# A Mamba-2 and attention trunk: the gate blocks read x's tokens, or write their columns, in another order

## The chip, the cores and the metric

The kernel runs on one NeuronCore of one Trainium2 chip. The metric is device time in microseconds, the median of several runs of the same program. A profile is one execution, taken by the hardware profiler.

## What is computed

The reference is a two-layer decoder trunk on x of 256 tokens by 2048 channels. The first layer is a Mamba-2 mixer, the second a sliding-window attention; each ends in a LayerNorm. The change touches the first projection of the first layer alone, and of it the part called z:

```python
zxbcdt = x @ w_in                                  # x: 256 x 2048
z = zxbcdt[..., :D_INNER]                          # D_INNER = 4096
xbc = zxbcdt[..., D_INNER:D_INNER + CONV_DIM]      # x, B and C of the state-space part
...
y = y.reshape(bsz, seqlen, D_INNER) * jax.nn.silu(z.astype(jnp.float32))
yg = y.reshape(bsz, seqlen, SSM_GROUPS, D_INNER // SSM_GROUPS)
yg = yg * lax.rsqrt(jnp.mean(jnp.square(yg), axis=-1, keepdims=True) + EPS)
```

So z is 4096 channels by 256 tokens, and silu of z gates the state-space output y, channel by channel and token by token.

## The kernel before

All weights come from HBM as fp32, in units of 128 x 2048. `load_unit` brings a unit in two DMAs (tile `wr`), ScalarE rounds it to fp32r (L133, tile `wh`) and VectorE takes the remainder (L134, tile `wl`). x is split once in the same way into `xH` and `xL`. A product is then three matmuls in `mac` (L195 to L197): high by high, high by low, low by high, all summed in PSUM.

The projection runs in eight groups of ten blocks. A block is one unit of weights, 128 output channels: for each of the 16 tiles of 128 input channels, `mac` holds 128 x 128 weights in the array and streams the 256 tokens of x, so a block is 48 matmuls of 256 columns into one PSUM tile `mm` (a ring of four). Channels lie on partitions and tokens along the row. The blocks of a group are B, C, four of xs and four of z (numbers 6 to 9, which the code calls i = 0 to 3); in group 0 the z blocks come first, and the very first of them shares its loop with the block of dt while the weights still come in. x lies in SBUF as rows of 256 fp32r tokens for each tile of 128 channels (`Split`), so a matmul of L195 reads 1024 contiguous bytes of each partition.

B, C and xs go through a short convolution (`conv_silu`: L357 on ScalarE, three L359 on VectorE). A z block goes through `in_z`: ScalarE reads PSUM and writes tanh to SBUF (L428), VectorE reads that and PSUM and makes the silu (L429). GpSimd multiplies y with z later (`gate`, L492). Between the blocks of groups 1 to 7 stand the output projection's units of the group before (`out_unit`, L255 to L257, 24 matmuls of 512 columns, added to `xr` by VectorE in L262).

The instructions are put in order on each engine by a scheduler that reads priorities; `in_z` is recorded with a raised priority (ZPRI). Group tasks (`cb`, `tr`, `ymm`, `gate`, `norm`) are placed behind given blocks by a table. Units are loaded two ahead of their use.

Of the kernel before, what the change touches and what calls it, by code (L numbers as in the profile page):

```python
# [11 lines left out]
AF = mybir.ActivationFunctionType  # L12
ALU = mybir.AluOpType
AX = mybir.AxisListType

P = 128
S = 256
D = 2048
KT = D // P
# [16 lines left out]
BLOCKS = list(range(10))  # L36
BLOCKS0 = [6, 7, 8, 9, 0, 1, 2, 3, 4, 5]
# [20 lines left out]
def trunk(ctx: ExitStack, tc: tile.TileContext, A: dict, out: bass.AP, dbg=None):  # L58
    nc = tc.nc
# [16 lines left out]
    def nm(s):  # L76
        uid[0] += 1
        return f"{s}_{uid[0]}"

    def mm_tile():  # L80
        return mm_ps.tile([P, 512], F32, tag="mm", name=nm("mm"), bufs=4)
# [38 lines left out]
    def load_unit(src, places):  # L120
        u = new_unit(places)
        raws = []
        for c in range(2):
            raw = wp.tile([P, 1024], F32, tag="wr", name=nm("wr"), bufs=NR)
            nc.sync.dma_start(raw[:], src[:, c * 1024 : (c + 1) * 1024])
            raws.append(raw)
        for c in range(2):
            for (h, k0, k1), (l, _, _) in zip(*u.parts):
                a, b = max(k0, 8 * c), min(k1, 8 * c + 8)
                if a < b:  # L130
                    sl = slice((a - k0) * P, (b - k0) * P)
                    raw = raws[c][:, (a - 8 * c) * P : (b - 8 * c) * P]
                    nc.scalar.activation(h[:, sl], raw, AF.Copy)  # L133
                    nc.vector.tensor_tensor(l[:, sl], raw, h[:, sl].bitcast(F32), ALU.subtract)  # L134
        return u

    def load_first():

        us = [new_unit([WHOLE, WHOLE]) for _ in range(2)]
        for k0, k1 in FIRST:  # L140
            n = k1 - k0
            if n < 3:
                raw = wp.tile([P, 2, 512], F32, tag="wr", name=nm("first"), bufs=NR)
            else:
                raw = ap.tile([P, 3, 512], F32, tag="e", name=nm("first"), bufs=2)
            raw = raw[:, :n, :]
            nc.sync.dma_start(raw, A["first"][:, k0:k1, :])
            nc.scalar.activation(xH(k0, k1), raw[:, :, :S], AF.Copy)
            nc.vector.tensor_tensor(xL(k0, k1), raw[:, :, :S], xH(k0, k1).bitcast(F32), ALU.subtract)
            for i, u in enumerate(us):  # L150
                h, l = [p[:, k0 * P : k1 * P].rearrange("p (k c) -> p k c", c=P) for p in (u.h, u.l)]
                w = raw[:, :, S + i * P : S + (i + 1) * P]
                nc.scalar.activation(h, w, AF.Copy)  # L153
                nc.vector.tensor_tensor(l, w, h.bitcast(F32), ALU.subtract)
        return us
# [23 lines left out]
    def next_unit():  # L179
        if not units:  # L180
            units.extend(load_first())
            nc.sync.dma_start(pc[:], A["pc"])
        while len(units) < min(used[0] + 1 + AHEAD, len(srcs)):
            if len(units) == 5:
                nc.sync.dma_start(cc[:], A["cc"])
            if len(units) in (8, 9):
                i = len(units) - 8
                nc.sync.dma_start(xr[:, i, :], A["xk"][:, i, :])
                nc.scalar.activation(xr[:, i, :], xr[:, i, :], AF.Copy, scale=ALPHA)
            units.append(load_unit(srcs[len(units)], BROKEN if len(units) in broken else [WHOLE, WHOLE]))  # L190
        used[0] += 1
        return units[used[0] - 1]

    def mac(ps, ah, al, bh, bl, first, last):
        nc.tensor.matmul(ps, ah, bh, start=first, stop=False)  # L195
        nc.tensor.matmul(ps, ah, bl, start=False, stop=False)  # L196
        nc.tensor.matmul(ps, al, bh, start=False, stop=last)  # L197
# [49 lines left out]
    xH = Split("xH", 1, 0, 192)  # L247
    xL = Split("xL", 1, 64, 192)
# [17 lines left out]
    def out_last(aH, aL, rms, stats, done):  # L266
# [12 lines left out]
            stats(1, nb)  # L279
        done(1)  # L280

    def gemm_ws(us):
        pss = [mm_tile() for _ in us]
        for k0, k1 in FIRST:
            for ps, u in zip(pss, us):
                for k in range(k0, k1):
                    ks = slice(k * P, (k + 1) * P)
                    mac(
                        ps[:, :S], u.h[:, ks], u.l[:, ks], xH(k, k + 1)[:, 0, :], xL(k, k + 1)[:, 0, :],
                        k == 0, k == KT - 1,  # L290
                    )
        return pss
# [127 lines left out]
    def in_xs(g, i, ps):  # L420
        xs = ap.tile([P, S], F32, tag="sm", name=nm("xs"), bufs=NSM)
        conv_silu(ps, g * 6 + 2 + i, xs[:])
        gs[g].__dict__.setdefault("xs", {})[i] = xs

    def in_z(g, i, ps):
        z = ap.tile([P, S], F32, tag="zz", name=nm("z"), bufs=4)
        with tc.high_priority(ZPRI):
            nc.scalar.activation(z[:], ps[:, :S], AF.Tanh, scale=0.5)  # L428
            nc.vector.scalar_tensor_tensor(z[:], z[:], 1.0, ps[:, :S], ALU.add, ALU.mult)  # L429
        gs[g].__dict__.setdefault("z", {})[i] = z  # L430

    def cb(g):
# [91 lines left out]
    def group(g):  # L524
        for b in range(10):
            if g == 0 and b < NFIRST - 1:
                ps = first_ps[b + 1]
            else:
                ps = gemm_ws([next_unit()])[0]
            k = BLOCKS0[b] if g == 0 else BLOCKS[b]  # L530
            if k >= 6:
                in_z(g, k - 6, ps)
            elif k >= 2:
                in_xs(g, k - 2, ps)
            else:
                (in_b, in_c)[k](g, ps)
            for fn, *a in plan.pop(10 * g + b, ()):
                fn(*a)
            if b in OUT_AT[g]:
                out_units(g - 1, [OUT_AT[g].index(b)])  # L540
        if g == NG - 1:
            out_units(g - 1, [1])
            out_units(g - 1, [2, 3])
            for t in sorted(plan):
                for fn, *a in plan[t]:
                    fn(*a)
        elif g > 0:
            out_units(g - 1, range(len(OUT_AT[g]), 4))

    def out_units(g, nbs):  # L550
        for nb in nbs:
            u = next_unit()
            for h in range(2):
                out_unit(*gs[g].y, h, u, nb, False, gs[g].rms)

    first_ps = gemm_ws([next_unit() for _ in range(NFIRST)])

    for c0, c1 in ((PC_CONV, PC_CONV + 240), (PC_NW, PC_NW + 32)):
# [70 lines left out]
    for g in range(NG):  # L629
        group(g)  # L630
# [90 lines left out]
    for h in range(2):  # L721
        ps = mm_tile()
# [152 lines left out]
    for what, j in B_ORDER[:-1]:  # L875
# [5 lines left out]
        else:  # L881
            for nb in range(4):
                u = next_unit()
# [143 lines left out]
```

## Time and profile before

| what | value |
|---|---|
| runs | 1022.56, 1023.02, 1022.55 us (median 1022.56) |
| the profiled execution's span, first to last instruction | 1022.1 us (its time around that is not given apart; the median of the runs is 0.5 us above it) |
| TensorE matmuls, share of the span | 98% |
| VectorE, ScalarE, GpSimd | 76%, 55%, 9% |
| matmuls of the first projection | L195, L196, L197 on xH and xL, 1296 recorded of each |
| HBM read | 195.93 MB, 194 GB/s over the span |

A row of a group reads: line, engine, operation, what is written and read, shape, count, then busy us and mean ns of one, then the idle time of the engine just ahead and who ended it. A timeline row has start, duration, engine, line, operation. A matmul's duration is its latency: the next one starts long before it ends, so rates are read from the distance of starts.

### The profile page before, as it was taken

To read this page: it belongs to the slowest core of one execution; us is meant where nothing else is said; L and a number is where in the kernel's file an instruction comes from. 1 tells how busy PE (TensorE), PEld (TensorE's weight loads), DVE (VectorE), ACT (ScalarE), POOL (GpSimd) and SP (SyncE) were. 2 spreads that over 40 slices of the span, in tenths; PEclk is the share of its full clock that TensorE was granted. 3 is DMA by queue.
4 is the path that set the end of the run, shared out by engine and by line. 5 is a ranking of instruction groups with operands and counts; after the bars stand their busy time and mean duration, and the time that the engine had idled before them with its cause. 6 is when DMAs were issued, how large, how long until landed. Compare 5 with 4: busy or idle time off the path is not lost. (4 is left out here: it accounts for less than half of the span.)

```text
span 1022.1 us, 17627 instructions
## 1 busy us (share of the span) xinstructions
PE 1001.7 (98%) x7028; PEld 905.5 (89%) x7028; DVE 774.2 (76%) x1106; ACT 562.8 (55%) x924; POOL 89.8 (9%) x112
## 2 busy tenths in 40 slices
PE   7999999999999999999999999999999999999997
PEld 7999899999998998999999999868988879879975
DVE  6868887876886787696786787798577785785776
ACT  6585857637655655664663763535545453453642
POOL 0000303004003002100300300301000000000002
PEclk9999999999999999999999999999999999999999
DMA  8786676575666666656656556647655445545522
GB/s 308 249 299 246 204 245 195 171 233 169 211 218 191 218 195 204 205 188 202 208 179 218 156 190 210 227 146 232 197 167 169 156 140 183 173 140 183 194 96 82
DMA packets 57794, 199.31 MB, mean 195 GB/s; under 512 B 6304, under 2 KB 10672, under 8 KB 56944
## 3 DMA queue, kind: packets, MB, share of 16 engines
q1 hardware_dynamic: 56352, 192.14, 57.3%
q0 software_dynamic: 1072, 5.53, 1.5%
q8 instruction: 55, 0.90, 0.4%
q10 hardware_dynamic: 288, 0.52, 0.1%
q14 instruction: 27, 0.22, 0.1%
HBM read 195.93 MB, written 2.23 MB: 194 GB/s over the span
## 5 line engine op out<-in xcount | busy, mean ns | idle before, releaser
L134 DVE TENSOR_TENSOR wl<-wr,wh 128x1024 fp32r<-128x1024 f32 (+2 forms) x342 | 398.3, 1181 | 135.4 <-ACT wh L133 134.0
L133 ACT ACTIVATE wh<-wr 128x1024 fp32r<-128x1024 f32 (+2 forms) x342 | 337.4, 1011 | 238.9 <-PE mm L196 77.1
L195 PE MATMUL mm<-xH,wh 128*128 128x256 f32 x1296 | 361.2, 279 | 8.0 <-ACT wh L153 6.0
L197 PE MATMUL mm<-xH,wl 128*128 128x256 f32 x1296 | 359.8, 278 | 2.1 <-DVE wl L134 2.1
L196 PE MATMUL mm<-xL,wh 128*128 128x256 f32 x1296 | 360.1, 278 | 0.0
L195 PEld LDWEIGHTS mm<-xH,wh 128*128 128x128 f32 x1296 | 244.6, 189 | 10.2 <-ACT wh L153 6.3
L197 PEld LDWEIGHTS mm<-xH,wl 128*128 128x128 f32 x1296 | 244.5, 189 | 2.7 <-DVE wl L134 2.7
L196 PEld LDWEIGHTS mm<-xL,wh 128*128 128x128 f32 x1296 | 244.7, 189 | 1.1
L255 PE MATMUL mm<-wh,yH 128*128 128x512 f32 x256 | 101.4, 396 | 0.0
L256 PE MATMUL mm<-wh,yL 128*128 128x512 f32 x256 | 99.9, 390 | 0.0
L257 PE MATMUL mm<-wl,yH 128*128 128x512 f32 x256 | 99.7, 390 | 0.0
L492 POOL TENSOR_TENSOR yz<-yz,z 128x256 f32<-128x256 f32 x32 | 32.9, 1036 | 532.0 <-DVE yz L487 532.0
L195 PE MATMUL mm<-x1H,wh 128*128 128x256 f32 x256 | 71.9, 281 | 0.0
L197 PE MATMUL mm<-x1H,wl 128*128 128x256 f32 x256 | 71.0, 277 | 0.0
L196 PE MATMUL mm<-x1L,wh 128*128 128x256 f32 x256 | 71.0, 277 | 0.0
L359 DVE SCALAR_TENSOR_TENSOR cv<-mm,pc,cv 128x255 f32<-128x255 f32 x144 | 68.6, 476 | 1.4
L712 PE MATMUL mm<-wh,x1H 128*128 128x512 f32 x160 | 63.3, 396 | 0.0
L714 PE MATMUL mm<-wl,x1H 128*128 128x512 f32 x160 | 62.6, 392 | 0.3 <-DVE wl L134 0.2
L713 PE MATMUL mm<-wh,x1L 128*128 128x512 f32 x160 | 62.6, 391 | 0.2 <-DVE x1L L676 0.2
L255 PEld LDWEIGHTS mm<-wh,yH 128*128 128x128 f32 x256 | 48.1, 188 | 10.3 <-DVE z L429 1.0
L257 PEld LDWEIGHTS mm<-wl,yH 128*128 128x128 f32 x256 | 48.1, 188 | 10.2
L256 PEld LDWEIGHTS mm<-wh,yL 128*128 128x128 f32 x256 | 48.1, 188 | 9.0
(180 smaller groups left out, 1306.2 us busy)
## 6 DMA issues: line engine op xcount, KB each, us to landing
wr<-in_wa SPq DMA_DIRECT2D x158, 512.0 KB, 5.0
wr<-in_wo SPq DMA_DIRECT2D x64, 512.0 KB, 4.8
wr<-in_wq SPq DMA_DIRECT2D x32, 512.0 KB, 4.5
wr<-in_wg SPq DMA_DIRECT2D x32, 512.0 KB, 5.2
wr<-in_wb SPq DMA_DIRECT2D x32, 512.0 KB, 4.6
rb<-rscr SPq DMA_DIRECT2D x16, 512.0 KB, 5.4
el<-rscr SPq DMA_DIRECT2D x16, 256.0 KB, 4.8
wr<-in_wkv SPq DMA_DIRECT2D x8, 512.0 KB, 4.3
```

Of the source, the lines that this page charges most:

```text
L133: nc.scalar.activation(h[:, sl], raw, AF.Copy)
L134: nc.vector.tensor_tensor(l[:, sl], raw, h[:, sl].bitcast(F32), ALU.subtract)
L195: nc.tensor.matmul(ps, ah, bh, start=first, stop=False)
L196: nc.tensor.matmul(ps, ah, bl, start=False, stop=False)
L197: nc.tensor.matmul(ps, al, bh, start=False, stop=last)
L255: nc.tensor.matmul(ps[:], aH[:, k, hs], u.h[:, ks], start=k == 0, stop=False)
L256: nc.tensor.matmul(ps[:], aL[:, k, hs], u.h[:, ks], start=False, stop=False)
L257: nc.tensor.matmul(ps[:], aH[:, k, hs], u.l[:, ks], start=False, stop=k == 3)
L359: nc.vector.scalar_tensor_tensor(a[:, sft:], ps[:, : S - sft], w(3 - sft), a[:, sft:], ALU.mult, ALU.add)
L712: nc.tensor.matmul(ps[:], x1H[:, kk, hs], u.h[:, ks], start=kk == 0, stop=False)
L713: nc.tensor.matmul(ps[:], x1L[:, kk, hs], u.h[:, ks], start=False, stop=False)
L714: nc.tensor.matmul(ps[:], x1H[:, kk, hs], u.l[:, ks], start=False, stop=kk == KT - 1)
```

## The change

The z blocks, but for the first, get a loop of their own, `gemm_z`. By i it differs in one thing:

- i = 0 streams the even tokens of x first and then the odd ones (`even_odd`, a step of 8 bytes). PSUM then holds even tokens, then odd ones. ScalarE and VectorE read it in one piece and write z with a step of two.
- i = 1 streams runs of 16 tokens (64 bytes), every second run first (`by_lines`). ScalarE and VectorE take each half of 128 columns in an instruction of its own and write it to its places in z.
- i = 2 streams x as before, but the matmuls write PSUM in that order: the first 128 tokens go to every second run of 16 columns, the others between them. ScalarE and VectorE read each half from its runs and write 128 contiguous columns of z.
- i = 3 stays as it was.

The values of z and their places in SBUF are the same as before.

```diff
+    def even_odd(v):
+        return v.rearrange("p (s r) -> p r s", r=2)
+
+    def by_lines(v):
+        return v.rearrange("p (c r s) -> p r c s", r=2, s=16)
+
+    def plain(v):
+        return v
+
+    ORDERS = [(even_odd, plain), (by_lines, plain), (plain, plain), (plain, plain)]
+
+    def gemm_z(u, i):
+
+        ps = mm_tile()
+        seen = ORDERS[i][0]
+        to = by_lines(ps[:, :S]) if i == 2 else ps[:, :S]
+        for k in range(KT):
+            ks = slice(k * P, (k + 1) * P)
+            xh, xl = xH(k, k + 1)[:, 0, :], xL(k, k + 1)[:, 0, :]
+            mac(to, u.h[:, ks], u.l[:, ks], seen(xh), seen(xl), k == 0, k == KT - 1)
+        return ps
...
-    def in_z(g, i, ps):
+    def in_z(g, i, ps, asis):
         z = ap.tile([P, S], F32, tag="zz", name=nm("z"), bufs=4)
+        if i == 2:
+            ls, lz = by_lines(ps[:, :S]), z[:].rearrange("p (r c s) -> p r c s", r=2, s=16)
+            pairs = [(ls[:, r, :, :], lz[:, r, :, :]) for r in range(2)]
+        elif i == 0 and not asis:
+            pairs = [(ps[:, :S].rearrange("p (r s) -> p r s", r=2), even_odd(z[:]))]
+        elif i == 1:
+            ls, lz = ps[:, :S].rearrange("p (r c s) -> p r c s", r=2, s=16), by_lines(z[:])
+            pairs = [(ls[:, r, :, :], lz[:, r, :, :]) for r in range(2)]
+        else:
+            pairs = [(ps[:, :S], z[:])]
         with tc.high_priority(ZPRI):
-            nc.scalar.activation(z[:], ps[:, :S], AF.Tanh, scale=0.5)
-            nc.vector.scalar_tensor_tensor(z[:], z[:], 1.0, ps[:, :S], ALU.add, ALU.mult)
+            for src, dst in pairs:
+                nc.scalar.activation(dst, src, AF.Tanh, scale=0.5)
+            for src, dst in pairs:
+                nc.vector.scalar_tensor_tensor(dst, dst, 1.0, src, ALU.add, ALU.mult)
...
-                ps = gemm_ws([next_unit()])[0]
+                k = BLOCKS0[b] if g == 0 else BLOCKS[b]
+                ps = gemm_z(next_unit(), k - 6) if k >= 6 and b > 0 else gemm_ws([next_unit()])[0]
...
-                in_z(g, k - 6, ps)
+                in_z(g, k - 6, ps, g == 0 and b == 0)
```

TensorE's instructions keep their places; the rows name the shape that is written, so there the blocks of i = 2 alone read differently (128x2x8x16 for 128x256). On VectorE, this is group 1 from its i = 0 block (z_1513) to the two sums of the out unit behind its i = 1 block (z_1626), before:

```order
L359 SCALAR_TENSOR_TENSOR cv_1442<-mm_1392,pc,cv_1442 128x253
L438 TENSOR_TENSOR cbm_1522<-ax_1523,cc 128x384
L429 SCALAR_TENSOR_TENSOR z_1513<-z_1513,mm_1464 128x256
L363 SCALAR_TENSOR_TENSOR xs_1441<-xs_1441,cv_1442 128x256
...
L429 SCALAR_TENSOR_TENSOR z_1626<-z_1626,mm_1577 128x256
L134 TENSOR_TENSOR wl_1686<-wr_1689,wh_1685 128x1024
L262 SCALAR_TENSOR_TENSOR xr<-mm_1657,r_1519,xr 128x512
L262 SCALAR_TENSOR_TENSOR xr<-mm_1671,r_1519,xr 128x512
```

And the same place after (lines and numbers of tiles are shifted):

```order
L381 SCALAR_TENSOR_TENSOR cv_1446<-mm_1396,pc,cv_1446 128x253
L472 TENSOR_TENSOR cbm_1526<-ax_1527,cc 128x384
L463 SCALAR_TENSOR_TENSOR z_1517<-z_1517,mm_1468 128x2x128
L385 SCALAR_TENSOR_TENSOR xs_1445<-xs_1445,cv_1446 128x256
...
L463 SCALAR_TENSOR_TENSOR z_1630<-z_1630,mm_1581 128x8x16 x2
L262 SCALAR_TENSOR_TENSOR xr<-mm_1663,r_1523,xr 128x512
L134 TENSOR_TENSOR wl_1692<-wr_1695,wh_1691 128x1024
L262 SCALAR_TENSOR_TENSOR xr<-mm_1677,r_1523,xr 128x512
```

The i = 0 block keeps one instruction and its place; the i = 1 block has two, and one half of a weight remainder (L134) has moved behind the first of the two sums. On ScalarE, the same group from its i = 1 block to its i = 2 block (z_1744), before:

```order
L428 ACTIVATE z_1626<-mm_1577 128x256
L133 ACTIVATE wh_1685<-wr_1689 128x1024
L133 ACTIVATE wh_1747<-wr_1749 128x1024
L133 ACTIVATE wh_1747<-wr_1751 128x1024
L133 ACTIVATE wh_1785<-wr_1787 128x1024
L428 ACTIVATE z_1744<-mm_1695 128x256
```

And after:

```order
L461 ACTIVATE z_1630<-mm_1581 128x8x16 x2
L133 ACTIVATE wh_1691<-wr_1695 128x1024
L133 ACTIVATE wh_1755<-wr_1757 128x1024
L133 ACTIVATE wh_1755<-wr_1759 128x1024
L133 ACTIVATE wh_1793<-wr_1795 128x1024
L461 ACTIVATE z_1750<-mm_1701 128x128 x2
```

Nothing changes its place there: two instructions of half the columns stand where one stood, ahead of the same splits of weights. GpSimd's and the DMA queue's rows are the same as before.

## The prediction

> **What bounds the kernel now.** I read the page's busy shares first, then its groups, then one window by stage, then the timeline of TensorE alone.
>
> ```profile
> span 1022.1 us, 17627 instructions
> PE 1001.7 (98%) x7028; PEld 905.5 (89%) x7028; DVE 774.2 (76%) x1106; ACT 562.8 (55%) x924; POOL 89.8 (9%) x112
> PEclk9999999999999999999999999999999999999999
> L195 PE MATMUL mm<-xH,wh 128*128 128x256 f32 x1296 | 361.2, 279 | 8.0 <-ACT wh L153 6.0
> L197 PE MATMUL mm<-xH,wl 128*128 128x256 f32 x1296 | 359.8, 278 | 2.1 <-DVE wl L134 2.1
> L196 PE MATMUL mm<-xL,wh 128*128 128x256 f32 x1296 | 360.1, 278 | 0.0
> 126.00:690.00 564.00, 561.02 (x4163) 521.02 (x4162) 438.85 (x584) 320.57 (x471) 68.83 (x84) 1.00 0.62 199
> ```
>
> TensorE holds 98% of the span, at a granted clock of 0.9 or more throughout. The last row (PE, PEld, DVE, ACT, POOL busy, then clock and DMA share) is the stretch with groups 1 to 7: TensorE 561.0 of 564, VectorE 438.9, ScalarE 320.6, DMA 0.62. So time put on a z block's matmuls goes onto the end almost one for one, and a few microseconds on the other two engines do not. The 279 ns of one matmul is a latency; matmuls overlap, and their price is the distance between starts:
>
> ```profile
> 207.19 0.39 PE L255 MATMUL mm<-wh,yH 128*128 128x512 f32 x1
> ...
> 212.42 0.39 PE L257 MATMUL mm<-wl,yH 128*128 128x512 f32 x1
> 212.64 0.28 PE L195 MATMUL mm<-xH,wh 128*128 128x256 f32 x1
> ...
> 213.35 0.28 PE L195 MATMUL mm<-xH,wh 128*128 128x256 f32 x1
> ...
> 215.96 0.28 PE L197 MATMUL mm<-xH,wl 128*128 128x256 f32 x1
> ```
>
> The 24 matmuls of two out tiles lie 23 steps from 207.19 to 212.42: 0.2274 us for 512 columns. In the next block the 24 from 213.35 to 215.96 lie 2.61/23 = 0.1135 us apart for 256 columns, and the six ahead of them (212.64 to 213.35) 0.118. So a step is proportional to the columns, 0.445 ns each, with no fixed part. These are fp32r operands, rounded halves of fp32. Plain fp32 matmuls are in the trace too:
>
> ```profile
> 91.80 1.04 PE L453 MATMUL ax<-cc,xs 128*128 128x128 f32 x8
> L453 PE MATMUL ax<-cc,xs x64: 270/272/273, 91.8 to 616.0; 128*128 128x128 f32 x64
> 1012.13 1.02 PE L905 MATMUL ax<-gb,cc 1*128 1x512 f32 x2
> 1012.56 1.02 PE L905 MATMUL ax<-gb,cc 1*128 1x512 f32 x2
> ```
>
> Eight of 128 columns take (1.04 - 0.272)/7 = 0.110 us each, one of 512 takes 0.43: (0.43 - 0.110)/384 = 0.833 ns a column. Half of that is 0.417, so fp32r runs at 0.445/0.417 = 1.07 of a clean half, about one slot in 16 lost. My reading (an inference) is that 4 bytes in every slot is just more than the supply of the moving operand gives, so this stream is already at its limit.
>
> **The change, part by part.** PE's rows keep their places. The first z block (asis) and all blocks of i = 3 stay as they were: 7 blocks of i = 0, 8 of i = 1 and 8 of i = 2 change, each of 16 x 3 = 48 matmuls.
>
> *i = 0, every second token first:* 7 x 48 = 336 matmuls read with an 8-byte step. No row has a stepped moving operand. Lower bound 0: the elements are as many. Upper bound: as if the skipped elements were streamed too, the 512-column row in place of the 256-column one, 0.2274 - 0.1135 = 0.1139 us, or 38.3 us in all. I take the upper one, because the lost sixteenth says that the supply already limits at step one, and a step of two draws half as much use from each piece of it. [...] No run here shows which.
>
> *i = 1, runs of 16 tokens, every second run first:* 384 matmuls. Each run is 64 contiguous bytes, so nothing fetched is wasted. Taken as 0; bounds are the 0.118 us of a block's first steps (384 x 0.0045 = 1.7 us) above and the lost sixteenth below (384 x (0.1135 - 256 x 0.000417) = 2.6 us of gain).
>
> *i = 2, the same runs written to PSUM:* 384 matmuls. Every write row of the trace is contiguous. Taken as 0, nearest to the rows of contiguous writes since 16 neighbours stay together; bounds 2.6 us of gain and a doubling, 384 x 0.1139 = 43.7 us.
>
> *ScalarE and VectorE.* Blocks of i = 1 and 2 issue two half instructions for one on each:
>
> ```profile
> L428 ACT ACTIVATE z<-mm 128x256 f32<-128x256 f32 x32 | 11.7, 366 | 1.5 <-PE mm L197 1.3
> L398 ACT ACTIVATE e<-rb,rtk 128x256 f32<-128x256 f32 x64 | 31.9, 498 | 0.0
> L398 ACT ACTIVATE e<-rb,rtk 128x128 f32<-128x128 f32 x64 | 25.0, 391 | 0.0
> L429 DVE SCALAR_TENSOR_TENSOR z<-z,mm 128x256 f32<-128x256 f32 x32 | 13.3, 414 | 4.1 <-ACT z L428 3.8
> L438 DVE TENSOR_TENSOR cbm<-ax,cc 128x384 f32<-128x384 f32 x8 | 4.4, 549 | 0.0
> PE mm L195 <- DVE cv L359: 1.9, 2, 1.3
> ```
>
> On ScalarE 128 columns less save 498 - 391 = 107 ns, so a half costs 366 - 107 = 259 and two cost 518: +152 x 16 = 2.4 us. On VectorE 549 - 414 = 135, a half 279, two 558: +144 x 16 = 2.3 us. Both lie beside TensorE, with 244 and 125 us to spare in the stretch above. Behind the extra instructions stand splits of weights (L133, L134) and the evacuations L262; TensorE waits for them only if they are late, and the PSUM ring has four tiles. Without that cover 16 x 0.296 = 4.7 us, so 0 to 4.7, taken as 0. Their strided reads and writes (i = 0 in one instruction each) cost at most one more duration, 7 x (0.366 + 0.414) = 5.5 us, under the same cover.
>
> *What goes.* The last row above is TensorE waiting for cv (1.3 us the longest), just behind the first changed i = 0 block:
>
> ```profile
> 123.99 0.36 ACT L428 ACTIVATE z<-mm 128x256 f32<-128x256 f32 x1
> 125.63 0.35 PE L195 MATMUL mm<-xH,wh 128*128 128x256 f32 x1 [1.32 <-DVE cv L359]
> 118.50 1.23 DVE L134 TENSOR_TENSOR wl<-wr,wh 128x1024 fp32r<-128x1024 f32 x1 [0.81 <-ACT wh L133]
> 120.82 1.22 DVE L134 TENSOR_TENSOR wl<-wr,wh 128x1024 fp32r<-128x1024 f32 x1 [1.10 <-ACT wh L133]
> ```
>
> If that block takes 48 x 0.114 = 5.5 us longer, VectorE, which itself idled 0.81 and 1.10 there, has cv done first, and 1.3 us go; nothing else is late there by the waits.
>
> Sum: +38.3 - 1.3 = +37.0 on the span, 1022.1 to 1059.1; the median of the runs is 0.5 above the profiled span, so **1059.6 us**, own range 1057 to 1063.
>
> **The rivals.** [...]
>
> *A slot per boundary.* The lost sixteenth is 0.1135 - 256 x 0.000417 = 0.0068 us a matmul, one slot each 16 elements (64 bytes). If it is paid at each such boundary, i = 0 crosses twice as many, and pays 336 x 0.0068 = 2.3 us: 1024.9. With blocks stuck at the 0.118 step, 1.5 more each for i = 0 and 1.7 for i = 1 and 2; if the step only partly starves, up to about half of the 38, 1042. For it: it needs only what is seen. Against it: nothing ties the loss to a place.
>
> *Broken writes to PSUM are dear.* i = 2 doubles: 1022.6 + 43.7 = 1066 alone, 1103 with the forecast. [...] Against it: no write row is slower than another.
>
> *Skipping pays.* If the lost sixteenth comes from taking neighbouring 64-byte pieces in turn, reading or writing alternate ones loses it: 384 x 0.0068 = 2.6 us for one of the two kinds, 5.2 for both, 1017.4 to 1020.0. Against it: it needs a conflict between neighbours that no row shows.
>
> **How the numbers follow.** Forecast 0.50, a slot per boundary or partly starved 0.16, free 0.18, dear writes 0.10 (half of it alone), skipping pays 0.06. Runs of this kernel lie within 0.05%, so 0.2% (2 us) is about what can be told. Slower: 0.50 + 0.10, 0.14 of the boundary case and 0.02 of the free one (halves exposed): 0.76. Same: 0.16 + 0.02 = 0.18. Faster 0.06. The range 1021.5 to 1066 leaves out skipping (0.06), dear writes on top of the forecast (0.05) and edges.
>
> **What would show it.** In the profile after, the steps of the z blocks: 0.227 us for i = 0 and 0.1135 for i = 1, 2 and 3 prove the forecast; the wait for cv near 125 us is gone; two instructions of about 259 and 279 ns stand where one of 366 and 414 stood. It is wrong if i = 0 steps at 0.1135 or 0.120, or if i = 1 or 2 leaves 0.11.

## The result, and the profile after

| | before | after |
|---|---|---|
| median of 4 runs | 1022.79 us (1022.55 to 1023.53) | 1063.62 us (1062.86 to 1064.54) |
| ratio | 1 | 1.0402, 95% interval 1.0385 to 1.0418 |
| span of the profiled execution | 1022.1 us | 1061.3 us |

The kernel became 4% slower. These are the page's lines after the change, first the busy shares, then the three groups of matmuls of the first projection:

```profile
span 1061.3 us, 17669 instructions
PE 1044.7 (98%) x7028; PEld 940.1 (89%) x7028; DVE 776.4 (73%) x1122; ACT 564.5 (53%) x940; POOL 89.8 (8%) x112
L195 PE MATMUL mm<-xH,wh 128*128 128x256 f32 x1296 | 376.7, 291 | 6.9 <-ACT wh L153 6.1
L197 PE MATMUL mm<-xH,wl 128*128 128x256 f32 x1296 | 375.7, 290 | 1.0 <-DVE wl L134 0.9
L196 PE MATMUL mm<-xL,wh 128*128 128x256 f32 x1296 | 376.0, 290 | 0.0
```

TensorE's share is 98% as before: all the new time is TensorE at work. VectorE grew by 2.2 us and ScalarE by 1.7, with 16 more instructions each. The mean of 279 ns became 291, which tells little, because it mixes blocks and is a latency. The starts tell where it went. TensorE's timeline, in group 2: a block of i = 0 (first pair of rows), of i = 1 (second) and of i = 2 (third):

```profile
205.26 0.41 PE L197 MATMUL mm<-xH,wl 128*128 128x256 f32 x1
...
215.58 0.41 PE L197 MATMUL mm<-xH,wl 128*128 128x256 f32 x1
...
221.67 0.29 PE L195 MATMUL mm<-xH,wh 128*128 128x256 f32 x1
...
227.01 0.29 PE L197 MATMUL mm<-xH,wl 128*128 128x256 f32 x1
...
228.37 0.28 PE L195 MATMUL mm<-xH,wh 128*128 128x256 f32 x1
...
233.37 0.28 PE L197 MATMUL mm<-xH,wl 128*128 128x256 f32 x1
```

There are 45 steps in the first pair, 10.32 us, so 0.2293 each. In the second and third there are 44: 5.34 us or 0.1214 each, and 5.00 us or 0.1136. In groups 1 to 6 every block of its kind reads the same within 0.001 us, and i = 3 is at 0.1138. So the step of two tokens doubled the matmuls of i = 0, the runs of 16 cost 0.0076 us each in i = 1, and the broken writes of i = 2 cost nothing.

The instructions of `in_z` after, by their shapes (line, engine, operation, count, busy us, mean ns):

```profile
L463 DVE SCALAR_TENSOR_TENSOR z<-z,mm 128x128 f32<-128x128 f32 x32 | 7.9, 283 | 0.6
L461 ACT ACTIVATE z<-mm 128x128 f32<-128x128 f32 x32 | 6.9, 267 | 1.4 <-PE mm L197 1.4
L463 DVE SCALAR_TENSOR_TENSOR z<-z,mm 128x256 f32<-128x256 f32 x16 | 6.7, 416 | 2.6 <-ACT z L461 2.6
L461 ACT ACTIVATE z<-mm 128x256 f32<-128x256 f32 x16 | 6.0, 374 | 0.0
```

A half costs 267 ns on ScalarE and 283 on VectorE (259 and 279 were worked out), and a write of z with a step of two costs next to nothing (374 and 416 ns as means of 7 stepped writes and 9 plain ones, 366 and 414 before; so about 18 and 5 ns for a stepped one). And from TensorE's waits (us in total, times, longest), the two that changed most:

```profile
PE mm L197 <- DVE wl L134: 0.9, 2, 0.7
PE mm L195 <- DVE cv L381: 0.7, 1, 0.7
```

The second was 1.9 us before, and the wait near 125 us is gone from it; the first was 2.1. What shrank of the first lies early; this is one of its waits, before and then after:

```profile
62.98 0.39 PE L197 MATMUL mm<-xH,wl 128*128 128x256 f32 x1 [0.76 <-DVE wl L134]
```

```profile
62.11 0.39 PE L197 MATMUL mm<-xH,wl 128*128 128x256 f32 x1 [0.20 <-DVE wl L134]
```

The other one that shrank, 0.49 us at 81 us, is gone. Both stand ahead of the first slowed block, which starts at 111 us, so the slow blocks did not remove them.

The sum closes: 336 x (0.2293 - 0.1135) = 38.9 us, 384 x 0.0076 = 2.9 us, less 1.2 us of waits for cv and 1.2 for wl, is 39.4 us; the span grew by 39.2. Single waits elsewhere that moved by up to half a microsecond are not in it.

### The profile page after: what moved, and what is told of

Read it like the earlier page. It is cut to its first block, busy times and chain, and to the rows that moved or that the text cites. A ratio compares the mean times of both kernels' runs of the same rounds, so it can differ in the third digit from the quotient of the medians.

```text
span 1061.3 us, 17669 instructions
## 1 busy us (share of the span) xinstructions
PE 1044.7 (98%) x7028; PEld 940.1 (89%) x7028; DVE 776.4 (73%) x1122; ACT 564.5 (53%) x940; POOL 89.8 (8%) x112
## 4 chain that ended last, share of the span: by engine, by line
PE 82%; DVE 6%; DMA 4%; ACT 4%; issue 2%; POOL 1%; SPq 0%; ACTq 0%; DVEq 0%; POOLq 0%
PE mm L195 15%; PE mm L196 15%; PE mm L197 15%; PE mm L255 7%; PE mm L256 7%; PE mm L257 7%; PE mm L747 3%; PE mm L748 3%; PE mm L749 3%; DVE wl L134 2%; ACT wh L133 2%; PE ax L510 2%; DMA wr<-in_wa 1%; PE ax L839 1%; PE ax L886 1%
## 5 line engine op out<-in xcount | busy, mean ns | idle before, releaser
L134 DVE TENSOR_TENSOR wl<-wr,wh 128x1024 fp32r<-128x1024 f32 (+2 forms) x342 | 398.8, 1183 | 161.4 <-ACT wh L133 159.5
L195 PE MATMUL mm<-xH,wh 128*128 128x256 f32 x1296 | 376.7, 291 | 6.9 <-ACT wh L153 6.1
L197 PE MATMUL mm<-xH,wl 128*128 128x256 f32 x1296 | 375.7, 290 | 1.0 <-DVE wl L134 0.9
L196 PE MATMUL mm<-xL,wh 128*128 128x256 f32 x1296 | 376.0, 290 | 0.0
L262 DVE SCALAR_TENSOR_TENSOR xr<-mm,r,xr 128x512 f32<-128x512 f32 x64 | 47.0, 744 | 14.7 <-PE mm L257 14.3
```

## The experiments

The names of orders are written alike in all of them: `(r, s)` is every r-th run of s tokens first, then the next ones. `READ` is the order in which x streams, `WRITE` the order of the columns in PSUM, one entry for each of i = 0 to 3; ScalarE and VectorE put z back in order in each. The fences show only the lines that set the order; the helper functions that carry it out are the same in all. Where one run is given, its time alone says little: 13 runs of the kernel before spread over 4.2 us. There the steps of its trace decide.

**e1, the step of two alone.**

```diff
-    ORDERS = [(even_odd, plain), (by_lines, plain), (plain, plain), (plain, plain)]
+    READ = [(2, 1), None, None, None]
+    WRITE = [None, None, None, None]
```

> The i = 0 blocks of groups 1 to 7 read the even tokens first, all other z blocks are as before. Theory (the price is TensorE's alone and adds up block by block): 336 matmuls at 0.2295 us instead of 0.1135, +39.0 us, less about 1.3 us of waits that go, 1060 to 1062 us. Rival (the two kinds of blocks and the split instructions hinder each other, so that either alone costs less than its share): under 1057 us.

Measured: 1061.28 us (1061.06 to 1061.66) against 1023.90 on the same chip (13 runs, 1021.54 to 1025.71), ratio 1.0367 (1.0349 to 1.0385). The i = 0 blocks step at 0.2295 us, all other z blocks at 0.1138. The theory holds (1060 to 1062 us), and the rival, under 1057, falls.

**e2, the runs of 16 alone, read in i = 1 and written in i = 2.**

```diff
+    READ = [None, (2, 16), None, None]
+    WRITE = [None, None, (2, 16), None]
```

> The i = 1 blocks read runs of 16 tokens, the i = 2 blocks write runs of 16 columns, i = 0 and 3 are as before. Theory: 384 matmuls at 0.1214 us instead of 0.1138, +2.9 us, and nothing for the written runs: 1025 to 1026 us. Rival (the 32 more instructions on ScalarE and VectorE delay TensorE too): 4.7 us more, 1030 us. Other rival (the slow step of i = 1 is an after-effect of the slow i = 0 block ahead of it): 1022.6 us.

Measured: 1026.52 us (1024.86 to 1027.67) against the same 1023.90, ratio 1.0022 (1.0012 to 1.0032). i = 1 steps at 0.1214 us again, with no slow block ahead of it, so it is no after-effect. The total is half a microsecond above the theory's 1025 to 1026, and the rival at 1030 us lies outside the measured range. The parts add up within the noise: +37.4 and +2.6 are 40.0 us, and both together are 40.8. And 384 x 0.0076 = 2.9 us already covers the 2.6, so nothing shows of the 32 extra instructions of ScalarE and VectorE. The interval leaves 1.2 to 3.3 us, so a cost of a few tenths could hide in it.

**e3, how long a run must be.** All z blocks read every second run first.

```diff
+    READ = [(2, 2), (2, 4), (2, 8), (2, 32)]
```

> All z blocks but the first read every second run of tokens first; the runs are 2, 4, 8 and 32 tokens for i = 0, 1, 2, 3. Steps per matmul. Theory A (the operand comes in 64-byte pieces and each piece touched costs 17 slots): 0.227 to 0.230 us for runs of 2, 4 and 8, 0.113 to 0.121 for 32. Theory B (16-byte pieces): 0.227 to 0.230 for runs of 2 alone, 0.113 to 0.13 for the rest. Theory C (two neighbouring words are fetched at a time): 0.113 to 0.13 for all four. Theory D (every break in the row costs about one slot of 0.42 to 0.5 ns, which fits 16 breaks at +0.008 and 256 at +0.116): 0.17, 0.145, 0.129 and 0.117.

TensorE's timeline, group 3, 44 steps in each pair: runs of 2, then of 4.

```profile
293.34 0.41 PE L197 MATMUL mm<-xH,wl 128*128 128x256 f32 x1
...
303.43 0.41 PE L196 MATMUL mm<-xL,wh 128*128 128x256 f32 x1
...
309.60 0.28 PE L197 MATMUL mm<-xH,wl 128*128 128x256 f32 x1
...
314.81 0.28 PE L196 MATMUL mm<-xL,wh 128*128 128x256 f32 x1
```

Runs of 2 step at 10.09/44 = 0.229 us, runs of 4 at 5.21/44 = 0.1184; in the other blocks of this run, 32 step at 0.1200, and 8 at 0.1198 in groups 2 to 6, where the block follows another z block, and at 0.1168 in groups 1 and 7, where an output unit stands between. So the step goes with what stands ahead of the block, by 3%; why is open. The slow rate ends between 2 and 4 tokens, 8 and 16 bytes: theory B's place, with 16 bytes as the piece. Theory A (64 bytes), C (pairs) and D (a slot for each break, which had fitted both blocks of the change) all fall. The kernel took 1064.44 us in one run, against 1023.90.

**e4, longer steps.**

```diff
+    READ = [(4, 1), (8, 1), (2, 64), (16, 1)]
```

> z blocks read single tokens with a step: 4 for i = 0, 8 for i = 1, 16 for i = 3; i = 2 reads runs of 64. Steps per matmul. Theory A (64-byte pieces): 0.45, 0.91 and 1.8 us. Theory B (16-byte pieces): 0.45 for all three. Theory C (pairs of words) and theory D (a slot for each break): 0.23 for all three. Runs of 64: 0.113 to 0.116 in each.

Group 3 again, the step of four and the step of sixteen, 44 steps each:

```profile
320.85 0.41 PE L197 MATMUL mm<-xH,wl 128*128 128x256 f32 x1
...
331.11 0.41 PE L196 MATMUL mm<-xL,wh 128*128 128x256 f32 x1
...
359.76 0.40 PE L197 MATMUL mm<-xH,wl 128*128 128x256 f32 x1
...
369.44 0.40 PE L196 MATMUL mm<-xL,wh 128*128 128x256 f32 x1
```

They step at 0.2332 and 0.2200 us, the step of eight at 0.2178, runs of 64 at 0.1140. Theories C and D, which fell in e3, expected 0.23 and had this right within 6%. B, which had e3 right, expected 0.45, with a piece fetched for every single token. So no theory had both. A token alone in its 16 bytes costs about as much as one of two (0.2332 and 0.229). So the price isn't the pieces fetched, as the prediction had put it. It reads as a rate: one token in one slot (the 0.44 ns that a column takes in order) when four neighbours come together, one in about two slots otherwise (0.85 to 0.91 ns). Runs of 3 were not tried. The kernel took 1140.36 us in one run, against 1023.90.

**e8, the same runs off by 8 bytes.** This asks whether the pattern in the instruction sets the rate, or the place in memory.

```diff
-    xH = Split("xH", 1, 0, 192)
-    xL = Split("xL", 1, 64, 192)
+    xH = Split("xH", 1, 8, 200)
+    xL = Split("xL", 1, 72, 200)
...
+    READ = [(2, 4), (2, 8), (2, 16), None]
```

> x lies 8 bytes higher in SBUF, so that runs start in the middle of 16 bytes. i = 0 reads runs of 4 tokens, i = 1 of 8, i = 2 of 16, i = 3 in order. Steps per matmul. Theory M (what counts is a whole aligned 16-byte piece of memory read in one go; its halves cost two slots an element): 0.229 us for runs of 4, 0.17 for 8, 0.145 for 16, 0.114 to 0.12 in order. Rival I (what counts is the pattern of the instruction, runs of four or more at step one): as when aligned, 0.1185, 0.1198, 0.1214 and 0.114.

Group 3, 44 steps in each pair: runs of 4, of 8, of 16, and in order.

```profile
310.70 0.41 PE L197 MATMUL mm<-xH,wl 128*128 128x256 f32 x1
...
320.77 0.41 PE L196 MATMUL mm<-xL,wh 128*128 128x256 f32 x1
...
327.08 0.34 PE L197 MATMUL mm<-xH,wl 128*128 128x256 f32 x1
...
334.74 0.34 PE L196 MATMUL mm<-xL,wh 128*128 128x256 f32 x1
...
336.25 0.31 PE L197 MATMUL mm<-xH,wl 128*128 128x256 f32 x1
...
342.63 0.31 PE L196 MATMUL mm<-xL,wh 128*128 128x256 f32 x1
...
348.63 0.28 PE L197 MATMUL mm<-xH,wl 128*128 128x256 f32 x1
...
353.90 0.29 PE L196 MATMUL mm<-xL,wh 128*128 128x256 f32 x1
```

They are 0.2289, 0.1741, 0.1450 and 0.1198 us. Runs of 4 that were fast at a 16-byte boundary (0.1184) are slow 8 bytes off it, where each is cut in 2 and 2. Runs of 8 are cut in 2, 4, 2, half their tokens slow: (0.1138 + 0.2295)/2 = 0.172. Runs of 16 have a quarter slow: 0.143. That the row merely starts off its place is not the cause: in order it starts 8 bytes off too, and steps at 0.1198. Rival I falls, and theory M is shown, within 3% of each step: what counts in these runs is an aligned 16-byte piece of memory, taken whole. (The traces hold no addresses; that x's rows start at such a boundary in the kernel before follows from runs of 4 being fast there.) The kernel took 1108.11 us in one run, against 1022.24.

**e6, a step of two in plain fp32.**

```diff
-        nc.tensor.matmul(ps[:, :256], st.bt[:, :128], st.ct[:], start=True, stop=True)
+        nc.tensor.matmul(ps[:, :256], st.bt[:, :128], order(st.ct[:], (2, 1)), start=True, stop=True)
```

> x is read in order everywhere. In the two matmuls of B and C (plain fp32, 256 columns, 0.216 us to the next before) the moving operand of the first is read with a step of two tokens. Theory (a step gives one element in two slots, and plain fp32 takes two slots a column anyway): 0.215 to 0.23 us still, nothing to be told in the whole. Rival (a step doubles a matmul whatever its type): 0.43 us.

TensorE's timeline of before, then of e6, in group 3; the first row of each is the fp32 product of 256 columns, which stands as two instructions, and the second what follows:

```profile
271.50 0.68 PE L436 MATMUL ax<-ct,bt 128*128 128x256 f32 x2
272.01 0.38 PE L437 MATMUL ax<-ct,bt 128*128 128x128 f32 x2
```

```profile
269.92 0.70 PE L474 MATMUL ax<-ct,bt 128*128 128x256 f32 x2
270.45 0.38 PE L475 MATMUL ax<-ct,bt 128*128 128x128 f32 x2
```

The pair took 0.51 us in order and 0.53 with the step: 0.01 us for each instruction, not 0.11. From the second of the two to the next instruction it is 0.216 us and 0.227. The theory holds: a product that takes 0.216 us for 256 columns in order, nearly twice the 0.1138 of fp32r, has room for nearly all of the step. (VectorE's product behind it, cbm, is done in two pieces here to put the columns back in order; that is not in the fence.) The whole took 1023.17 us in one run, against 1022.24.

**e5, shorter runs in PSUM.**

```diff
+    READ = [None, None, None, None]
+    WRITE = [(2, 2), (2, 4), (2, 8), (4, 2)]
```

> x is read in order everywhere. The z blocks write PSUM in every second run first: runs of 2, 4 and 8 columns for i = 0, 1, 2, and every fourth run of 2 for i = 3. Steps per matmul. Theory W (a written run of 2 columns, 8 bytes, is enough): 0.1135 to 0.114 us in all four, about 1023 us in all. Rival (PSUM needs 16 bytes in a row, as the read side does): 0.22 to 0.23 for i = 0 and 3, 0.114 for the others, 1100 us. Other rival (any break in a write costs a slot): 0.167, 0.14, 0.127, 0.167.

The i = 0 block of group 2, written in runs of 2, from its fourth matmul to its last, 44 steps:

```profile
202.70 0.28 PE L195 MATMUL mm<-xH,wh 128*128 128x256 f32 x1
...
207.71 0.28 PE L197 MATMUL mm<-xH,wl 128*128 128x256 f32 x1
```

That is 5.01/44 = 0.1139 us. All four kinds step at 0.1138 us in nearly every group, in whatever runs they write. Theory W holds: 8 bytes in a row are enough. Single columns were not tried. The kernel took 1026.54 us in one run, against 1022.24, and not about 1023, though its matmuls are as fast as before. Its waits of TensorE:

```profile
PE mm L195 <- DVE cv L387: 3.1, 3, 1.5
PE mm L197 <- DVE wl L134: 2.6, 3, 1.0
```

They were 1.9 and 2.1. Here 47 more instructions stand on each of ScalarE and VectorE than before, where the change has 16. By these two lines TensorE waits 1.7 us more, of 2.7 on the span, which suggests that some of that now reaches it. It is not shown: in e2, with 16 more, the same lines read 2.6 and 1.7, and in e6, with the z blocks as before, 1.6 and 1.6.

**e7, x moved by 64 bytes.**

```diff
-    xH = Split("xH", 1, 0, 192)
-    xL = Split("xL", 1, 64, 192)
+    xH = Split("xH", 1, 0, 128)
+    xL = Split("xL", 1, 64, 128)
...
+    READ = [None, (2, 16), None, None]
```

> i = 1 reads runs of 16; all other blocks read in order. x lies 64 bytes lower in SBUF against the weights, but for the first of its 16 tiles. Theory P (the 8 ns of i = 1 are meetings of the moving stream with the weight loads, which go by the place of both): the step of i = 1 leaves 0.1214 us by more than 1 ns, and the steps of the blocks in order may leave 0.1138 as well. Rival (a break costs half a slot by itself): 0.1214 and 0.1138 stay.

Group 3, 44 steps in each pair: i = 1 with its runs of 16, then i = 3 in order.

```profile
299.11 0.28 PE L195 MATMUL mm<-xH,wh 128*128 128x256 f32 x1
...
304.40 0.28 PE L197 MATMUL mm<-xH,wl 128*128 128x256 f32 x1
...
316.87 0.28 PE L195 MATMUL mm<-xH,wh 128*128 128x256 f32 x1
...
322.10 0.28 PE L197 MATMUL mm<-xH,wl 128*128 128x256 f32 x1
```

Over the groups, i = 1 steps at 0.1200 us and the blocks in order at 0.1187, so 0.1214 and 0.1138 both moved, and the price of the runs fell from 0.0076 to 0.0013 us; one run took 1038.06 us against 1022.24. The rival falls. Theory P is borne out as far as this: the small price goes by where x lies, and reading in order is fastest at the place that x had, of the three tried here. Whether it is x's place against the weights or its place as such no run tells apart, and that the meeting partner is the weight load was only argued.

## Why the prediction was right, and where it wasn't

*The bound.* That TensorE's time goes onto the end one for one held: 41.8 us of longer matmuls, 39.2 on the span. (The row read as groups 1 to 7 starts at 126 us, while group 1 starts at 74.6; it leaves out most of group 1, the first slowed block included.)

*i = 0.* The deciding choice, the upper bound of 38.3 us, measured 38.9. That a stepped operand comes slower was right; why was not. I had priced it as if the skipped elements were streamed too, each fetched piece being used half as well, and by that a step of four would cost twice as much again. It costs the same (0.2332). The rate has two levels (0.1135 to 0.1214 us a step in whole pieces at the place that x had, 0.2178 to 0.2332 for single tokens and runs of 2). At a step of two, half the use and half the rate give the same number, so that the size came out so well is in part luck. The lost sixteenth, on which I had rested the choice, is not explained by this: it is there in runs that fill their pieces (0.1138 us in order, where half the plain fp32 price would be 0.1067), and stays open. (The 128-column rows of L453 from which plain fp32 was priced are transposes; L436, a product, gives the same price, 0.216 us for 256 columns.)

*That stepped reads are free*, which had a chance of 0.18, fell with the first i = 0 block: it stepped at 0.2293 us and not at 0.1135. For this stream two neighbouring words are not enough (runs of 2 step at 0.229), four are (0.1184). In plain fp32, at little more than half the rate, a step of two is nearly free (0.01 us more on 0.216). *A slot per boundary* fell with the same block (0.0068 us expected, 0.116 found), and its variant, a slot for each break, in e3, where a break at every 4 tokens cost 0.005 us and not 0.03.

*i = 1* is the term that was mis-sized: taken as 0 with 1.7 us as the upper end, it cost 2.9. By the prediction's own sign (it is wrong if i = 1 leaves 0.11) this part was wrong, and whole aligned pieces are not all that counts, as e7 shows. The bound came from a block's first steps (0.118), the only sign in the trace of such slips, and a larger one (0.1214) was possible.

*i = 2* at 0 was right (0.1136 us a step), down to runs of 2 columns. *Broken writes to PSUM are dear* fell with the i = 2 blocks, and e5 contradicts it for shorter runs too (0.1138 us in runs of 2 columns with gaps), though no run writes single columns.

*ScalarE and VectorE* at 0 were right for 16 extra instructions each, as far as e2 can tell; e5 hints that with 47 they begin to show.

*What goes.* 1.3 us for cv was right in kind (0.7 of 1.9 stays) and short in size: 1.2 us of waits for wl went as well, though not through the slow blocks (e1 has the same slow blocks and keeps 2.0 of the 2.1 us).

*The median* lies 4.0 us above the forecast and 0.6 above its own range: 2.2 from the span (2.9 + 0.6 - 1.1 more waits gone, within 0.2), the rest because the runs lie 2.3 us above the profiled span, not 0.5. In every execution on record the time is 1.7 to 1.9 us above the span of the same execution. So the profiled execution of before was itself some 1.3 us longer than the median of the runs, and the 0.5 that the prediction added came out of that.

## What to carry to other kernels

Stream a matmul's fp32r operand in whole, aligned 16-byte pieces: four neighbouring words that start at a multiple of 16 bytes from where x's rows start here (runs of 4 stepped at 0.1184 us there, and at 0.2289 with x moved by 8 bytes). Steps of 2, 4, 8 and 16 words (0.2295, 0.2332, 0.2178 and 0.2200 us), runs of 2 words (0.229) and pieces cut by an 8-byte offset (0.2289) all about doubled the time of the elements they touch (0.1138 in order), while the order of whole pieces cost at most 7% (0.1214), and the order of the columns in PSUM, down to pairs, nothing (0.1138). If an order has to change, change it in how runs of four or more are visited, or on the engine that evacuates PSUM (a stepped write of 256 columns cost about 18 ns there). To price a matmul in a trace, divide the distance between two starts by the matmuls between them, block by block; the mean duration of 291 ns hid a doubling.

## What was not expected of the hardware

- A step of 4, 8 or 16 words costs about the same as a step of 2: 0.233, 0.218 and 0.220 us against 0.2295 for 256 columns.
- Runs of 16 words, in whole 16-byte pieces, cost 7% more than reading in order at the place that x had (0.1214 against 0.1138 us), runs of 64 nothing (0.1140), and moving x by 64 bytes alone makes reading in order 4% slower (0.1187).
- With x moved by 8 bytes reading in order is slower too: 0.1198 us.
- Blocks of one kind in one run stepped at 0.1168 us behind an output unit and at 0.1198 behind another z block (runs of 8 in e3).
